# x in four large loads and transposed unscaled, and load buffers of w_ada and of the weights kept apart

## The chip, the cores and the metric

The kernel runs on one core of one Trainium2 chip. The metric is the device time of one execution in microseconds. The engines are TensorE (PE, with its weight loads as PEld), VectorE (DVE), ScalarE (ACT), GpSimd (POOL) and SyncE (SP), whose queue issues nearly all DMAs.

## The reference, cut to what matters

One decoder layer over x of 256 rows by 2048 columns, in float32:

```python
mod = jax.nn.silu(c) @ w_ada + b_ada                  # 2048 x 6144
shift, scale, gate = jnp.split(mod, 3, axis=-1)
h = _rms_norm(x, g_norm) * (1.0 + scale[:, None, :]) + shift[:, None, :]
proj = h @ w_in                                       # 2048 x 9296
qa, ka, va, za, q_idx, k_idx, w_idx, qb, kb, vb, zb = jnp.split(proj, COL_SPLITS, axis=-1)
...
ya = _dsa_attention(qa, ka, va, q_idx, k_idx, w_idx, _alibi_slopes(N_HEADS_A))
yb = _moba_attention(qb, kb, vb, _alibi_slopes(N_HEADS_B))
ya = ya.reshape(B, L, D_A) * jax.nn.silu(za)
yb = yb.reshape(B, L, D_B) * jax.nn.silu(zb)
y = jnp.concatenate([ya, yb], axis=-1) @ w_out        # 2048 x 2048
return x + gate[:, None, :] * y
```

Each of the two attentions has 8 heads of 128. The first attends to the top 64 keys of an indexer's score, the second is causal over the whole sequence.

## The kernel before

**Three matrix stages, one stream of loads.** w_ada (50 MB), w_in (76 MB) and w_out (17 MB) are each read once. A list `loads`, made by a planner at the top of the kernel, gives their order; SP issues them in it. A load of w_ada is a row of the transposed matrix for each of 128 partitions (128 x 2048, 1 MB): DVE multiplies it by `s_row` (the silu of c, the same in all partitions) and sums along the row (`gemv`, L274), which gives 128 values of shift, scale or gate. A load of w_in or w_out holds up to four k tiles (rows of 128) of one group of 512 columns (`za1`, `qb0`, ...; three groups `i0` to `i2` are narrower). A quad load holds one k tile of the four groups z, q, k, v of one half of the heads.

**Products in three passes.** Matmuls are done in a rounded float32 type. So each weight pair of k tiles is split: ACT rounds it (`wh`, L315, `cast_hi`), DVE subtracts that from the original (`wl`, L328, `cast_lo`), and PE adds three products for each k tile and each half t of the rows (L775 `wh` x `hhi`, L776 `wl` x `hhi`, L777 `wh` x `hlo`). The casts are written two pairs ahead of the matmuls (`LA`).

**h comes in chunks.** x is loaded, normalised by its row (`rx`), and transposed in 16 blocks of 128 columns (`xnT`). A chunk of one or two k tiles of h (`build_h`) needs two or four loads of w_ada; its ACT and DVE instructions make `hhi` and `hlo`. The planner places the w_ada loads at fixed distances, in k tiles of work (`ADA_NEXT`, `ADA_GAP`), and lets a projection start on the k tiles that are known, so that many groups are summed in several segments, each added to `p_...` by DVE or copied by ACT. Chunk 0 (k tile 0) starts the kernel: `start_mod` and a part of `build_h` turn five partial sums into its shift and scale.

**Buffers.** All loads share one ring of four buffers of 1 MB (`rawp`); a load is issued when the one four before it in the list has been read:

```python
raw = rawp.tile([P, 2048], F32, tag="raw", name=f"raw{n_issued}")
```

The rounded weights lie in two rings of four tiles, `wh` and `wl`. Numbers in names such as `raw6` are places in `loads`; numbers in `wh6` count pairs.

**Order.** A scheduler orders each engine's instructions by what it reckons, except inside `with in_order()`, which keeps the order of the code on each engine; the start is written so. Attention heads, gates and `build_h` are background steps that a small queue (`Bg`) mixes in between pairs. Each gate's `build_gate` waits some steps between its sum and its PE transposes (`yield 2`).

Of the kernel before, what the change touches and what calls it, by code (L numbers as in the profile page):

```python
# [13 lines left out]
P = 128  # L14
# [38 lines left out]
def hybrid_block(ctx: ExitStack, tc: tile.TileContext, x, cols, w_ada_t, w_in, w_out, out):  # L53
# [4 lines left out]
    rawp = ctx.enter_context(tc.tile_pool(name="rawp", bufs=4))  # L58
# [126 lines left out]
    while turn:  # L185
# [12 lines left out]
        if g[0] == "z" and end == seg0 + 1 and [pos[o] for o in gs] == 4 * [seg0]:  # L198
# [6 lines left out]
            first = len(loads) == len(PARTS)  # L205
            for lo, hi in ((0, 1), (1, 3), (3, 4)) if first else ((0, 2), (2, 4)):
                for i in range(lo, hi):
                    members[i]["pair"] = (lo, hi)
            loads.append(dict(kind="quad", quad=g[1:], k=seg0, members=members, first=first))
# [18 lines left out]
    for n, qs in seq:  # L228
        for q in qs:
            loads.append(w_load(w_out_r, f"o{n}", n * 512, 512, list(yk[q]), "y", q == QUADS[0],  # L230
                                q == QUADS[-1], True, True))

    n_start = 2 * CHUNKS[0][1]
    n_issued = 0

    def issue(upto):
        nonlocal n_issued
        while n_issued < min(upto, len(loads)):
# [27 lines left out]
    def gemv(ld):  # L266
# [15 lines left out]
    ada_done = []  # L282

# [535 lines left out]
```

## Time and profile before

| | |
|---|---|
| median of 3 runs | 585.94 us (584.33 to 586.25) |
| the profiled execution | 584.79 us, with a span of 583.0 us in the trace |
| granted TensorE clock, mean | 0.996 |
| PE / PEld / DVE / ACT / POOL busy | 554.7 / 458.2 / 451.8 / 318.6 / 49.3 us |
| DMA traffic | 150.08 MB, mean 257 GB/s |

The profiled execution is 1.79 us longer than its span (what lies around it), and 1.15 us shorter than the median. Busy time of PE is modelled: a matmul that waits in the array's queue counts as busy, so the count of matmuls in a stretch says more than its busy share.

### The profile page before, as it was taken

The page shows a single profiled execution, that of the slowest core. Times are in us where ns is not written, and L with a number is a line of the kernel's source. Part 1 is how long each engine was busy: PE and PEld are TensorE (multiplying, and loading weights), DVE is VectorE, ACT ScalarE, POOL GpSimd, SP SyncE. Part 2 cuts the span into 40 slices and gives each one's busy share as a digit, 9 for nine tenths or more (in the row PEclk, how much of TensorE's full clock was granted, in tenths as well). Part 3 has the DMA queues.
Part 4 walks back from the last instruction along what each step waited for, and adds up shares of the span by engine and source line. Part 5 has one row for each costly group of instructions (what it writes and reads, how often), then busy time and mean ns, then how long its engine had stood idle before and what let it go on. Part 6 is the DMA issues. An engine that isn't in the chain of part 4 may idle for free.

```text
span 583.0 us, 7393 instructions
## 1 busy us (share of the span) xinstructions
PE 554.7 (95%) x2626; PEld 458.2 (79%) x2626; DVE 451.8 (77%) x698; ACT 318.6 (55%) x648; POOL 49.3 (8%) x66
## 2 busy tenths in 40 slices
PE   4887999999999999999999998999999999999996
PEld 3666688878898888787776887888888888888885
DVE  4796689899988887979978899997587556557452
ACT  5766645353545352536588675657755775544340
POOL 5400000000000000010021120111101110000000
PEclk9999899999999999999999999999999999999999
DMA  8889898999899979898666465877495459445701
GB/s 278 336 280 330 327 335 273 345 327 360 308 359 329 389 290 333 317 310 311 223 216 215 148 217 184 320 247 255 170 341 181 144 171 332 147 145 195 238 37 36
DMA packets 59973, 150.08 MB, mean 257 GB/s; under 512 B 3104, under 2 KB 9504, under 8 KB 54048
## 3 DMA queue, kind: packets, MB, share of 16 engines
q1 hardware_dynamic: 58784, 147.51, 72.2%
q10 hardware_dynamic: 1152, 2.10, 1.2%
q8 instruction: 20, 0.33, 0.2%
q14 instruction: 17, 0.14, 0.1%
HBM read 147.50 MB, written 2.10 MB: 257 GB/s over the span
## 4 chain that ended last, share of the span: by engine, by line
PE 70%; DVE 12%; ACT 7%; DMA 5%; issue 3%; POOL 2%; SPq 0%; DVEq 0%; ACTq 0%
PE mm_y_o L775 5%; PE mm_y_o L777 5%; PE mm_y_o L776 5%; DVE wl L328 5%; DVE raw L274 3%; DMA raw<-in_w_in 3%; ACT wh L315 3%; PE mm_h_i L775 2%; PE mm_h_ka L775 2%; PE mm_h_va L777 2%; PE mm_h_va L776 2%; PE mm_h_qa L777 2%; PE mm_h_ka L777 2%; PE mm_h_ka L776 2%; PE mm_h_i L776 2%
## 5 line engine op out<-in xcount | busy, mean ns | idle before, releaser
L315 ACT ACTIVATE wh<-raw 128x1024 fp32r<-128x1024 f32 (+3 forms) x189 | 186.7, 1003 | 164.5 <-DMA raw<-in_w_in 58.3
L328 DVE TENSOR_TENSOR wl<-raw,wh 128x1024 fp32r<-128x1024 f32 (+3 forms) x189 | 214.6, 1153 | 71.5 <-ACT wh L315 70.8
L274 DVE CUSTOM_DVE_ANT_0 raw<-raw,s_row 128x2048 f32<-128x2048 f32 (+2 forms) x51 | 110.9, 2177 | 8.4 <-DMA raw<-in_w_ada_t 8.3
L775 PE MATMUL mm_y_o<-wh,yT 128*128 128x512 f32 x128 | 51.5, 403 | 0.0
L777 PE MATMUL mm_y_o<-wh,yT 128*128 128x512 f32 x128 | 49.9, 390 | 0.0
L776 PE MATMUL mm_y_o<-wl,yT 128*128 128x512 f32 x128 | 49.9, 390 | 0.0
L775 PE MATMUL mm_h_i<-wh,hhi 128*128 128x384 f32 (+1 forms) x96 | 32.0, 335 | 3.2 <-DVE p_i L684 2.0
L776 PE MATMUL mm_h_i<-wl,hhi 128*128 128x384 f32 (+1 forms) x96 | 31.6, 330 | 0.8 <-DVE wl L328 0.8
L777 PE MATMUL mm_h_i<-wh,hlo 128*128 128x384 f32 (+1 forms) x96 | 31.4, 329 | 0.0
L777 PEld LDWEIGHTS mm_y_o<-wh,yT 128*128 128x128 f32 x128 | 24.0, 188 | 5.3 <-DVE yT L582 0.2
L775 PEld LDWEIGHTS mm_y_o<-wh,yT 128*128 128x128 f32 x128 | 24.1, 188 | 4.8 <-ACT yT L581 0.2
L776 PEld LDWEIGHTS mm_y_o<-wl,yT 128*128 128x128 f32 x128 | 24.1, 188 | 4.6
L775 PE MATMUL mm_h_qa<-wh,hhi 128*128 128x512 f32 x64 | 26.2, 412 | 1.1 <-ACT p_za L682 1.1
L775 PE MATMUL mm_h_zb<-wh,hhi 128*128 128x512 f32 x64 | 25.6, 405 | 1.5 <-ACT wh L315 1.5
L776 PE MATMUL mm_h_zb<-wl,hhi 128*128 128x512 f32 x64 | 25.9, 404 | 0.7 <-DVE wl L328 0.7
L775 PE MATMUL mm_h_kb<-wh,hhi 128*128 128x512 f32 x64 | 25.9, 410 | 0.6 <-ACT wh L315 0.6
L775 PE MATMUL mm_h_ka<-wh,hhi 128*128 128x512 f32 x64 | 25.9, 407 | 0.0
L775 PE MATMUL mm_h_vb<-wh,hhi 128*128 128x512 f32 x64 | 25.9, 407 | 0.0
L777 PE MATMUL mm_h_za<-wh,hlo 128*128 128x512 f32 x64 | 25.0, 392 | 0.9 <-DVE hlo L424 0.9
L775 PE MATMUL mm_h_za<-wh,hhi 128*128 128x512 f32 x64 | 25.8, 408 | 0.0
L777 PE MATMUL mm_h_zb<-wh,hlo 128*128 128x512 f32 x64 | 25.7, 401 | 0.0
L776 PE MATMUL mm_h_kb<-wl,hhi 128*128 128x512 f32 x64 | 25.2, 393 | 0.5 <-DVE wl L328 0.5
(225 smaller groups left out, 1209.5 us busy)
## 6 DMA issues: line engine op xcount, KB each, us to landing
raw<-in_w_in SPq DMA_DIRECT2D x50, 1024.0 KB, 5.8
raw<-in_w_ada_t SPq DMA_DIRECT2D x46, 1024.0 KB, 6.2
raw<-in_w_out SPq DMA_DIRECT2D x16, 1024.0 KB, 5.0
raw<-in_w_in SPq DMA_DIRECT2D x18, 512.0 KB, 3.9
raw<-in_w_in SPq DMA_DIRECT2D x11, 768.0 KB, 5.9
x<-in_x SPq DMA_DIRECT2D x8, 256.0 KB, 5.0
xr<-in_x ACTq DMA_DIRECT2D x8, 256.0 KB, 7.7
raw<-in_w_in SPq DMA_DIRECT2D x3, 672.0 KB, 4.3
```

What stands on the lines that cost most here:

```text
L274: nc.vector.tensor_tensor_reduce(out=ld["v"][:, h0:h1], in0=ld["v"][:, h0:h1], in1=s_row[:, h0:h1], scale=1.0, scalar=0.0, op0=ALU.mult, o ...
L315: nc.scalar.activation(hi[:, :n, :w], v, AF.Copy)
L328: nc.vector.tensor_tensor(lo[:, :n, :w], v, sb["hi"][:, :n, :w].bitcast(F32), op=ALU.subtract)
L775: nc.tensor.matmul(ps, a_hi, sb["hi"][:, sb["i"] + i, :w], start=st, stop=False)
L776: nc.tensor.matmul(ps, a_hi, sb["lo"][:, sb["i"] + i, :w], start=False, stop=False)
L777: nc.tensor.matmul(ps, a_lo, sb["hi"][:, sb["i"] + i, :w], start=False, stop=en)
```

## The change

**Loads.** The one ring of 1 MB buffers becomes two: two of 1 MB for w_ada and four of 512 KB for weights. Every weight load is now at most one pair of k tiles (a quad becomes two loads, the first quad three), so that a load and its pair of casts are one to one; 156 loads become 237. `issue` no longer follows the list alone: it takes, of the kinds that have a free buffer, the load that stands first in the list; a w_ada load only if it is at most four places ahead. A weight buffer counts as free after its `cast_lo`, a w_ada buffer after the next `cast_hi` behind its `gemv`. The planner asks for w_ada loads between pairs, no longer between fours. `wh` and `wl` become two halves of one tile.

**x.** Four loads of 512 KB take the place of eight of 256 KB. ACT squares all of them (four instructions of 1024 columns); one `rsqrt` serves both halves of the rows. Only block 0 is scaled before its transposes; the other 15 are transposed as they are. `rx` is itself transposed and copied over all partitions (`r_bc`), and POOL multiplies blocks 1 to 15 by it (`x_norm`), in places spread over the first pairs (`X_AT`). Blocks 1 to 7 get a copy from PSUM by ACT there (`x_copy`), where before `build_h` read PSUM itself.

**Smaller.** Chunk 0's partial sums are joined by DVE alone, with one instruction behind the last sum, not three on POOL and one on DVE. `build_gate` waits eight steps, not two.

```diff
-    rawp = ctx.enter_context(tc.tile_pool(name="rawp", bufs=4))
+    rawp = ctx.enter_context(tc.tile_pool(name="rawp", bufs=1))
...
+    def w_tile(name):
+
+        return wsp.tile([P, 2, 2, 512], F32R, tag="w", name=name)
...
-        for k in range(seg0, end, 4):
-            n = min(4, end - k)
+        for k in range(seg0, end, 2):
+            n = min(2, end - k)
...
+    AHEAD = 4
+    kinds = {kind: [n for n, ld in enumerate(loads) if (ld["kind"] == "ada") == (kind == "ada")] for kind in ("ada", "w")}
+    free = {"ada": 2, "w": 4}
...
+    def issue():
+        while True:
+            ns = [kinds[kind][0] for kind in kinds if kinds[kind] and free[kind] > 0
+                  and (kind == "w" or kinds[kind][0] <= next_load + AHEAD)]
+            if not ns:
+                break
+            n_issued = min(ns)
             ld = loads[n_issued]
-            raw = rawp.tile([P, 2048], F32, tag="raw", name=f"raw{n_issued}")
...
+            if kind == "ada":
+                raw = ld["v"] = rawp.tile([P, D], F32, tag="ada", bufs=2, name=f"ada{n_issued}")
...
+                raw = rawp.tile([P, 1024], F32, tag="raw", bufs=4, name=f"raw{n_issued}")
...
+            for n, (h0, h1) in enumerate(parts[:-1]):
+                part(h0, h1, 2 + n)
+            more = acc[:, 3:4] if len(parts) > 2 else 0.0
+            nc.vector.scalar_tensor_tensor(acc[:, 4:5], acc[:, 2:3], more, bmod[:, i:i + 1], op0=ALU.add, op1=ALU.add)
+            part(*parts[-1], i)
+            nc.vector.tensor_scalar(acc[:, i:i + 1], acc[:, i:i + 1], acc[:, 4:5], gcol[:, 0:1] if i else 1.0,
+                                    op0=ALU.add, op1=ALU.mult)
...
+        while read:
+            free[read.pop()] += 1
+        issue()
         flush_gemv()
...
-        lo = wsp.tile([P, 2, 512], F32R, tag="wl", name=f"wl{j}")
-        nc.vector.tensor_tensor(lo[:, :n, :w], v, sb["hi"][:, :n, :w].bitcast(F32), op=ALU.subtract)
-        sb["lo"] = lo
+        nc.vector.tensor_tensor(sb["lo"][:, :n, :w], v, sb["hi"][:, :n, :w].bitcast(F32), op=ALU.subtract)
+        free["w"] += 1
+        issue()
...
+    xt = [w_tile(f"x{t}").rearrange("p c k n -> p (c k n)").bitcast(F32) for t in range(2)]
     for t in range(2):
-        for j in range(4):
-            xx = u_tile(f"x_{t}_{j}")
-            nc.sync.dma_start(xx, x[t * P:(t + 1) * P, j * 512:(j + 1) * 512])
-            xt.append(xx)
-    issue(n_start + 1)
+        for h in range(2):
+            nc.sync.dma_start(xt[t][:, h * 1024:(h + 1) * 1024], x[t * P:(t + 1) * P, h * 1024:(h + 1) * 1024])
+    issue()
...
+    def x_norm(k):
+
+        nc.gpsimd.tensor_tensor(xnT[k], xnT[k], r_bc, op=ALU.mult)
...
-        yield 2
+        yield 8
...
+        for t in range(2):
+            nc.scalar.activation(xt[t][:, :P], xt[t][:, :P], AF.Copy, scale=rx[:, t:t + 1])
+        for t in range(2):
+            for k in range(8, 16):
+                x_transpose(k, t)
+        for t in range(2):
+            x_transpose(0, t)
+        for k in (8, 9, 10, 11, 0, 12, 13, 14, 15):
             x_copy(k)
+        for k in range(1, 8):
+            for t in range(2):
+                x_transpose(k, t)
+        pr = mm_tile("prx")
+        for t in range(2):
+            nc.tensor.transpose(pr[:, t * P:(t + 1) * P], rx[:, t:t + 1].to_broadcast([P, P]), ident)
...
+    X_AT = {1 + 2 * (k - 1): k for k in range(1, KT)}
...
+        if j in X_AT:
+            with in_order():
+                if X_AT[j] < 8:
+                    x_copy(X_AT[j])
+                x_norm(X_AT[j])
```

What this moves shows at three places. On ACT, at the start, from the scaling of x to the first weights (`xnT8` is block 8 of x transposed, `hhi0` the first tile of h, `r_bc` the row factors, the last `raw` and `w` rows are the weights of the first quad); before:

```order
L366 ACTIVATE x_1_3_162<-x_1_3_162,rx_175 128x512
L385 ACTIVATE xnT0_249<-ptx0_209 128x256
L385 ACTIVATE xnT8_251<-ptx4_215 128x256
...
L385 ACTIVATE xnT11_257<-ptx5_218 128x256
L315 ACTIVATE wh0_274<-raw2_171 128x512
L417 ACTIVATE hhi0_279<-xnT0_249,mmod0_259 128x256
L385 ACTIVATE xnT12_285<-ptx6_221 128x256
...
L385 ACTIVATE xnT15_291<-ptx7_224 128x256
L315 ACTIVATE wh1_293<-raw2_171 128x1024
```

and now:

```order
L638 ACTIVATE x1_149<-x1_149,rx_170 128x128
L387 ACTIVATE xnT8_208<-ptx4_185 128x256
...
L387 ACTIVATE xnT11_214<-ptx5_188 128x256
L387 ACTIVATE xnT0_216<-ptx0_205 128x256
L387 ACTIVATE xnT12_218<-ptx6_191 128x256
...
L387 ACTIVATE xnT15_224<-ptx7_194 128x256
L344 ACTIVATE w0_258<-raw2_161 128x512
L411 ACTIVATE hhi0_263<-xnT0_216,mmod0_246 128x256
L659 ACTIVATE r_bc_171<-prx_243 128x256
L344 ACTIVATE w1_272<-raw3_163 128x1024
```

All nine copies stand ahead of `hhi0`, and a copy of `r_bc`, which needs the last transposes of PE, stands between `hhi0` and the second weights.

On SP, the loads behind the first quad (a row that reads `in_w_ada_t` is a load of w_ada; the group of the next weights, `za1`, is `raw6` before and `raw9` now); before:

```order
L252 DMA raw3_268<-in_w_in 128x4x512
L244 DMA raw4_270<-in_w_ada_t 128x2048
L244 DMA raw5_272<-in_w_ada_t 128x2048
L260 DMA raw6_325<-in_w_in 128x2x512
L260 DMA raw7_383<-in_w_in 128x2x512
L244 DMA raw8_385<-in_w_ada_t 128x2048
L260 DMA raw9_387<-in_w_in 128x2x512
L244 DMA raw10_416<-in_w_ada_t 128x2048
L260 DMA raw11_434<-in_w_in 128x2x512
L260 DMA raw12_436<-in_w_in 128x2x336
```

and now:

```order
L260 DMA ada7_256<-in_w_ada_t 128x2048
L275 DMA raw6_261<-in_w_in 128x2x512
L260 DMA ada8_270<-in_w_ada_t 128x2048
L275 DMA raw9_275<-in_w_in 128x2x512
L275 DMA raw10_295<-in_w_in 128x2x512
L275 DMA raw12_312<-in_w_in 128x2x512
L275 DMA raw14_344<-in_w_in 128x2x512
L275 DMA raw15_379<-in_w_in 128x2x336
L260 DMA ada11_403<-in_w_ada_t 128x2048
L260 DMA ada13_405<-in_w_ada_t 128x2048
```

Five weight loads now stand ahead of the third and fourth w_ada load of this stretch (`ada11` and `ada13`, which were `raw8` and `raw10`), where one and two stood before.

On DVE, the same stretch (L274 and L289 are the products with w_ada, `hlo1` is the rest of the second tile of h, L328 and L354 the second casts); before:

```order
L328 TENSOR_TENSOR wl9_420<-raw7_383,wh9_418 128x1024
L408 TENSOR_TENSOR mmod1_389<-mmod1_389,cc_76 128x1
L680 COPY p_za0_1_432<-mm_h0_za0_1_423 128x512
L274 ISA raw8_385,mmod2_438<-raw8_385,s_row_110 128x2048
L274 ISA mmod2_438 128x1
L424 TENSOR_TENSOR hlo1_414<-xnT1_411,hhi1_410 128x256
L328 TENSOR_TENSOR wl10_442<-raw9_387,wh10_440 128x1024
```

and now:

```order
L679 COPY p_za0_1_422<-mm_h0_za0_1_413 128x512
L404 TENSOR_TENSOR mmod1_373<-mmod1_373,cc_76 128x1
L354 TENSOR_TENSOR w9_407<-raw10_295,w9_407 128x1024
L354 TENSOR_TENSOR w10_426<-raw12_312,w10_426 128x1024
L417 TENSOR_TENSOR hlo1_398<-xnT1_289,hhi1_395 128x256
L354 TENSOR_TENSOR w11_455<-raw14_344,w11_455 128x1024
L289 ISA ada11_403,mmod2_424<-ada11_403,s_row_110 128x2048
```

`hlo1` no longer stands behind the product with that w_ada load, and two casts have moved ahead of it.

## Rows read from the trace of the kernel before

**Rows 1.** The page: the chain that ended last, share of the span by engine.

```profile
PE 70%; DVE 12%; ACT 7%; DMA 5%; issue 3%; POOL 2%; SPq 0%; DVEq 0%; ACTq 0%
```

**Rows 2.** Windows: stretch, length, busy (count) by engine, PEclk, DMA share, GB/s.

```profile
21.60:40.00 18.40, 16.84 (x68) 12.23 (x68) 15.60 (x19) 14.45 (x26) 0.00 (x0) 1.00 0.75 266
40.00:56.00 16.00, 13.69 (x64) 10.93 (x64) 11.86 (x13) 10.27 (x18) 0.00 (x0) 1.00 0.92 323
56.00:70.00 14.00, 11.19 (x39) 8.03 (x38) 8.90 (x13) 9.09 (x14) 0.00 (x0) 0.88 1.01 389
70.00:130.00 60.00, 59.96 (x263) 49.21 (x263) 55.19 (x66) 29.11 (x39) 0.00 (x0) 1.00 0.89 310
...
250.00:350.00 100.00, 95.40 (x497) 76.92 (x496) 85.43 (x177) 66.21 (x184) 14.67 (x13) 1.00 0.68 232
```

**Rows 3.** The same view of three shorter stretches.

```profile
11.00:25.00 14.00, 9.96 (x42) 7.45 (x40) 10.07 (x20) 7.96 (x19) 7.42 (x8) 1.00 1.03 406
25.00:31.00 6.00, 6.00 (x28) 4.96 (x28) 5.62 (x6) 5.94 (x12) 0.00 (x0) 1.00 0.36 116
31.00:37.00 6.00, 4.85 (x22) 3.62 (x20) 6.00 (x9) 4.13 (x7) 0.00 (x0) 1.00 0.85 268
```

**Rows 4.** Timeline of SP's queue: start, length, what it issued.

```profile
25.85 4.67 SPq L260 DMA_DIRECT2D raw<-in_w_in  x2
31.28 0.34 SPq L244 DMA_DIRECT2D raw<-in_w_ada_t  x1
```

**Rows 5.** Timeline of the start: start, length, instruction, [idle before <-releaser].

```profile
14.88 1.33 ACT L366 ACTIVATE x<-x,rx 128x512 f32<-128x512 f32 x2 [3.40 <-POOL rx L139]
...
15.78 1.57 DVE L274 CUSTOM_DVE_ANT_0 raw<-raw,s_row 128x1024 f32<-128x1024 f32 x1
...
18.50 2.82 PE L377 MATMUL ptx<-ident,x 128*128 128x128 f32 x12 [0.19 <-POOL x L368]
18.91 0.08 DVE L274 DVE_READ_ACCUMULATOR2_ANT mmod<- 128x1 f32 x1
...
20.96 0.60 ACT L417 ACTIVATE hhi<-xnT,mmod 128x256 fp32r<-128x256 f32 x1
...
21.61 0.50 PE L775 MATMUL mm_h_qb<-wh,hhi 128*128 128x512 f32 x1 [0.30 <-ACT hhi L417]
...
23.66 0.73 PE L775 MATMUL mm_h_kb<-wh,hhi 128*128 128x512 f32 x2 [0.35 <-ACT wh L315]
```

**Rows 6.** Groups of instructions by form, 20 to 70 us: busy us, mean ns | idle before.

```profile
L274 DVE CUSTOM_DVE_ANT_0 raw<-raw,s_row 128x2048 f32<-128x2048 f32 x7 | 16.0, 2289 | 4.2 <-DMA raw<-in_w_ada_t 4.2
L328 DVE TENSOR_TENSOR wl<-raw,wh 128x1024 fp32r<-128x1024 f32 x12 | 14.5, 1222 | 7.0 <-ACT wh L315 7.0
L315 ACT ACTIVATE wh<-raw 128x1024 fp32r<-128x1024 f32 x12 | 12.6, 1062 | 2.4 <-DMA raw<-in_w_in 2.4
```

**Rows 7.** What PE waited for, 21.6 to 70 us, then 250 to 360: total, times, longest.

```profile
PE mm_h_zb L775 <- ACT wh L315: 1.5, 1, 1.5
...
PE mm_h_za L777 <- DVE hlo L424: 0.9, 1, 0.9
...
PE pgate L435 <- DVE ygb L578: 1.5, 1, 1.5
```

**Rows 8.** Timeline of DVE around the second tile of h.

```profile
38.13 2.29 DVE L274 CUSTOM_DVE_ANT_0 raw<-raw,s_row 128x2048 f32<-128x2048 f32 x1 [1.06 <-DMA raw<-in_w_ada_t]
...
40.35 0.42 DVE L424 TENSOR_TENSOR hlo<-xnT,hhi 128x256 fp32r<-128x256 f32 x1
```

**Rows 9.** Groups by form, 0 to 22 us: POOL's scaling of x, ACT's copies of blocks.

```profile
L368 POOL TENSOR_SCALAR x<-x,rx 128x512 f32<-128x512 f32 x3 | 4.7, 1573 | 0.0
...
L385 ACT ACTIVATE xnT<-ptx 128x256 f32<-128x256 f32 x8 | 2.5, 382 | 2.6 <-PE ptx L377 2.6
```

**Rows 10.** DMA issues, 70 to 250 us: count, KB each, median us to landing.

```profile
raw<-in_w_in SPq DMA_DIRECT2D x20, 1024.0 KB, 6.2
...
raw<-in_w_in SPq DMA_DIRECT2D x5, 512.0 KB, 5.4
```

More of the change, by code (lines that the diff above doesn't have):

```diff
@@ L204, in hybrid_block @@
                               end == KT) for c in "qkvz"]
-            first = len(loads) == len(PARTS)
-            for lo, hi in ((0, 1), (1, 3), (3, 4)) if first else ((0, 2), (2, 4)):
+            for lo, hi in ((0, 1), (1, 3), (3, 4)) if len(loads) == len(PARTS) else ((0, 2), (2, 4)):
                 for i in range(lo, hi):
-                    members[i]["pair"] = (lo, hi)
-            loads.append(dict(kind="quad", quad=g[1:], k=seg0, members=members, first=first))
+                    members[i]["i"] = i - lo
+                loads.append(dict(kind="quad", quad=g[1:], k=seg0, members=members[lo:hi], lo=lo, hi=hi))
             n_kt += 4
@@ L229, in hybrid_block @@
         for q in qs:
-            loads.append(w_load(w_out_r, f"o{n}", n * 512, 512, list(yk[q]), "y", q == QUADS[0],
-                                q == QUADS[-1], True, True))
+            for k in yk[q][::2]:
+                loads.append(w_load(w_out_r, f"o{n}", n * 512, 512, [k, k + 1], "y",
+                                    q == QUADS[0] and k == yk[q][0], q == QUADS[-1] and k == yk[q][2], True, True))
     n_start = 2 * CHUNKS[0][1]
[L234 to L238, printed above, removed]
-            ld = loads[n_issued]
-            raw = rawp.tile([P, 2048], F32, tag="raw", name=f"raw{n_issued}")
-            if ld["kind"] == "ada":
-                ld["v"] = raw
+    AHEAD = 4
@@ L270, in gemv, with part @@
             mod[kind, c] = work.tile([P, 8], F32, name=f"m{kind}{c}", tag="m" + kind)
-        for n, (h0, h1) in enumerate(ld.get("parts", [(0, D)])):
-            o = i if (kind, c) != ("mod", 0) else 2 * i + n
+        acc = mod[kind, c]
+        def part(h0, h1, o):
             nc.vector.tensor_tensor_reduce(out=ld["v"][:, h0:h1], in0=ld["v"][:, h0:h1], in1=s_row[:, h0:h1],
                                            scale=1.0, scalar=0.0, op0=ALU.mult, op1=ALU.add,
-                                           accum_out=mod[kind, c][:, o:o + 1])
-            if (kind, c, o) == ("mod", 0, 3):
-                start_mod()
+                                           accum_out=acc[:, o:o + 1])
+        parts = ld.get("parts")
+        if parts:
+            for n, (h0, h1) in enumerate(parts[:-1]):
[5 more added lines that the diff above has]
+                                    op0=ALU.add, op1=ALU.mult)
+        else:
+            part(0, D, i)
+        read.append("ada")
         if "end" in ld:
@@ L282, in hybrid_block @@
     ada_done = []
+    read = []
     subs = []
@@ L380, in hybrid_block, with x_transpose @@
-    for k in range(8):
-        xnT[k] = None
+        for h in range(2):
+            nc.sync.dma_start(xt[t][:, h * 1024:(h + 1) * 1024], x[t * P:(t + 1) * P, h * 1024:(h + 1) * 1024])
+    issue()
+    ssx = consts.tile([P, 2, 2], F32, name="ssx")
+    rx = consts.tile([P, 2], F32, name="rx")
+    r_bc = h_tile("r_bc")
+    xnT, ptx = {}, {}
+    def x_transpose(k, t):
+        k2, i = k // 2, k % 2
+        if k2 not in ptx:
+            ptx[k2] = ps_tile(("tr", "s", "pt", "pv")[k2], f"ptx{k2}") if k2 < 4 else mm_tile(f"ptx{k2}")
+        o = i * L + t * P
+        src = xt[t][:, k * P:(k + 1) * P]
+        nc.tensor.transpose(ptx[k2][:, o:o + P], src, ident)
@@ L659, in hybrid_block @@
             pass
-        for k in range(12, 16):
-            x_copy(k)
+        nc.scalar.activation(r_bc, pr[:, :L], AF.Copy)
     ada_done.remove(0)
@@ L678, in evac @@
                     proj[g, t] = u_tile(f"p_{g}_{t}")
-                    if "pair" in ld and t == 1 and ld["i"] == 1:
+                    if t == 1 and ld.get("i") == 1:
                         nc.vector.tensor_copy(proj[g, t][:, :w], ps[:, :w])
```

106 lines of the change are left out of this document (30 added, 76 removed).

## The prediction

> **What bounds the kernel now.** I read four views in this order. First the page's chain that ended last: PE carries 70% of it, DVE 12%, ACT 7%, DMA 5% [rows 1], so most of the time goes with PE's own pace, and a gain has to come from places where PE is not at work. The windows by stage say where those are. From 70 to 130 us PE has 263 matmuls in 60 us, one each 0.228 us, with no idle time [rows 2]; there nothing can be won but by PE. Between 21.6 and 70 us it has only 171 in 48.4 us [rows 2]. Of these, 36 are of the narrow groups i0 to i2 (three pairs of 12, 336 and 384 columns of 512, so about 0.165 us each); the rest at 0.228 gives 30.8 + 5.9 = 36.7 us. So 11.7 us are lost there, after the 21.6 us before the first product, and these two are what a change of the start can reach. Of the 11.7, some 1.7 are no wait: the granted clock has a mean of 0.88 from 56 to 70 us [rows 2], which is 12% of 14 us, so for a part of it the clock was at its lower level of 1.2 GHz, right behind PE's longest wait of the stretch, 1.5 us for the first cast of zb [rows 7].
>
> The third view is that of the DMAs in the same stretch. From 11 to 25 us they move 406 GB/s, then 116 up to 31 us and 268 up to 37 [rows 3]. SP shows why: its next weights go out only at 25.85 us, and the next load of w_ada at 31.28 [rows 4], since all four buffers are held by loads that have landed and wait for their casts. In those 12 us 2.3 MB moved where 4.9 could have, which is 6.3 us of transfer. The fourth view, DVE's and ACT's waits of 20 to 70 us, shows the bill: 4.2 us of waiting for w_ada and 2.4 for weights [rows 6].
>
> **The change, part by part.** *Start.* x has the same bytes and the same last landing, and ACT squares the last 1024 columns in about the time that DVE took; so I leave `rx` at 14.9 us, where ACT's scaling begins now [rows 5]. Then ACT scales two blocks (0.6), copies blocks 8 to 11 and 0 (five at no more than 0.38 [rows 9], 1.7 us): 17.2. The other transposes share a PSUM bank with block 0 and follow its copy: 14, and two of `rx`, at 2.82 / 12 = 0.235 us [rows 5], 3.8 us: 21.0. The first product, 21.61 now [rows 5], moves by 0.6. Chunk 0's numbers would be there earlier: the three POOL steps between the last sum at 18.99 and `hhi` at 20.96 go [rows 5], about 1.7 us, and that lead is lost behind the transposes. Next come the copy of `r_bc` (0.38) and the second weights' cast (1.06 [rows 6]), 22.4 for 23.66 [rows 5]. **-1.2 us**, between -2.0 and 0.
>
> *Loads.* The two rings take the first quads as four loads beside two of w_ada, and three pairs of weights follow as each small load is cast, not as a whole megabyte is. So weights of za1, qa1, ka1 stand in line 5 to 10 us before they do now, and `ada11` and `ada13` behind them. Two places gain. `hlo1` stands behind a product with w_ada that began late at 38.13 us, and starts at 40.35 [rows 8], while PE waits for it [rows 7]. It now stands behind one cast more and not behind that product: DVE is free at 38.13 - 1.06 = 37.07 [rows 8], one cast takes 1.22 [rows 6], so `hlo1` starts near 38.3: **-2.0 us** (0 if that cast's data are late, -3.3 if it is done before). And the weights of zb are in line before the last w_ada load of the next chunk, so the wait of 1.5 us and the lower clock behind it (1.7) should go: **-3.2 us** (0 to -8, all else that is lost up to 70 us).
>
> Loads of half the size cost 81 more issues on SP, of 0.34 us as the single one in [rows 4], spread over 570 us of a queue that mostly waits; nothing of it is late unless a load is. A 512 KB load took 5.4 us to land beside others, a 1024 KB one 6.2 [rows 10]; for bytes that is much worse, but several are in flight. A ring of four turns once in 5.4 + 1.06 + 1.22 + one product with w_ada in DVE's way, 2.29 [rows 6, 10] = 10.0 us; PE needs 4 x 12 x 0.228 = 10.9 us for four loads. Covered, by 0.9: **0**. The Trainium skill, DMA: Bandwidth & Descriptors, "Rules for kernel authors", asks for at least 1 MiB for each DMA. Its fixed 2.0 us a DMA ("Anatomy of one DMA") would be, as an estimate from that page, 162 us for 81 more loads if none overlapped and the sum near 740; the trace agrees on the direction (5.4 is far more than half of 6.2), not on the price, as loads overlap.
>
> *POOL's multiplies.* 15 new instructions of 128 x 256 with two inputs, between 23 and about 60 us. No row shows one. Beside POOL's scaling of x (1.57 us each [rows 9]) DVE's product of 1024 columns took 1.57 us [rows 5] where half of one of 2048 is 1.14 [rows 6]: 0.4 us of delay. I take that for each, the nearest row: 6.3 us of DVE. DVE is idle for 18.4 - 15.6 + 16 - 11.9 + 14 - 8.9 = 12 of the 48.4 us [rows 2], but not where the chain of w_ada, casts and h runs through it; I put a fifth on the path, **+1.2 us**, between 0 and 15 x 1.57 - 12 = 11.6. The Trainium skill, SBUF — State Buffer, "Who interferes with whom", says that a DVE instruction with two inputs in SBUF and a POOL instruction that reads SBUF lock each other out for a whole instruction. The trace agrees (1.57 against 1.14).
>
> *ACT* gets eight copies of 0.38 in place of five scalings: nothing, as it is idle for a quarter of that time [rows 2]; without that cover, 3 us.
>
> *Later.* Up to 250 us the order of loads is that of the list. From 250 to 350 us, 12 products for the gates stand before cast 133, where eight did, and DVE is busy for 85 of 100 us there [rows 2]; against that, the gates' transposes come six steps later, and PE now waits 1.5 us for one [rows 7]. **0**, between -1.5 and +2.3 (one product in a tight place).
>
> Sum: -1.2 - 2.0 - 3.2 + 1.2 = -5.2 us. The profiled execution, 584.8, would be 579.6; the median stands 1.15 above it: **580.7 us**, between 574 (all but a little of what is lost won) and 584.
>
> **The rivals.**
> 1. *Given back.* PE comes to 70 us five earlier, but DVE has 55 of 60 us of work there [rows 2], and every product with w_ada must come as much earlier. If DVE or the loads cannot, PE waits until it is where it was: 585, no change. For it: PE's waits end just as DVE saturates. Against it: DVE's idle 12 us before are what the earlier data fill.
> 2. *The ring is too short (slower).* All the weights in flight are 2 MB; before, up to four. Place: 70 to 240 us. If landings beside w_ada take 7.5 us and not 5.4, the ring turns in 12.1 us against 10.9, 11% of 170 us, 18 us lost: 599. It decides from a landing of 6.7 us on ((6.7 + 4.57 - 10.9) / 10.9 x 170 = 5.8, about the gain). For it: 6.2 us for the large ones [rows 10], and segments of five k tiles that split 2, 2, 1. Against it: w_ada no longer holds these buffers, and they come free after one cast, not two. By the rule of the Trainium skill on the size of a DMA (DMA: Bandwidth & Descriptors, "Rules for kernel authors") this rival is the one to expect.
> 3. *POOL's lock (slower).* If each multiply stops DVE for 1.57 us and DVE's idle time is all the cover, 11.6 us stand against 6.4: 591. It decides from (12 + 6.4) / 15 = 1.2 us each. Against it: the 0.4 seen, at twice the columns.
>
> **How the numbers follow.** A median of this kernel's runs can tell about 0.3%, 1.8 us, from no change. Forecast 0.62, given back 0.16, short ring 0.12, lock 0.10. All of the forecast's range is faster, both last rivals are mostly slower: faster 0.62, same 0.16, slower 0.22. 574 to 588 holds nearly all of the first two and the near part of the slower ones, about 0.8; the forecast's own range is 574 to 584.
>
> **What would show it.** Start: the first product near 21.0 us, the second group near 22.4. Loads: DMA from 25 to 37 us above 300 GB/s; `hlo1` near 38.3; no wait at zb and a granted clock of 1.00 from 50 to 70 us; more than 190 matmuls up to 70 us. Ring: from 70 to 240 us one matmul each 0.228 us as now, and 512 KB loads landing in under 6.7 us. Lock: DVE's products between 25 and 60 us not much over 2.7 us. It would be wrong if PE began to wait for casts after 70 us, if transposes of x held the first products past 21.6, or if the third and fourth load of w_ada, now behind five of weights, made the chunk after the second late enough that zb's wait only moves to qb.

## The result, and the profile after

The changed kernel takes 591.52 us (median of 4 runs, 589.81 to 593.28), the kernel before 585.56 us beside it. The ratio is 1.0104, with a 95% interval from 1.0080 to 1.0128: 6.1 us slower, where 580.7 us and faster were forecast. The profiled execution took 589.81 us, with a span of 588.0 us. The chain of the page has moved from PE towards the others, against [rows 1]:

```profile
PE 64%; DVE 13%; ACT 10%; issue 4%; DMA 4%; POOL 3%; SPq 0%; ACTq 0%; DVEq 0%
```

The windows by stage, as in [rows 2] (busy time and count of PE, PEld, DVE, ACT and POOL, granted clock, DMA share, GB/s), and under them those of [rows 3]:

```profile
21.60:40.00 18.40, 16.95 (x70) 12.38 (x69) 16.70 (x18) 16.56 (x31) 8.00 (x5) 1.00 0.83 310
40.00:56.00 16.00, 13.74 (x67) 11.23 (x65) 15.25 (x13) 8.92 (x18) 16.00 (x9) 1.00 0.96 354
56.00:70.00 14.00, 12.18 (x44) 9.28 (x45) 10.41 (x12) 7.68 (x12) 1.41 (x3) 0.88 0.77 267
70.00:130.00 60.00, 58.36 (x256) 47.39 (x255) 54.97 (x68) 28.22 (x37) 0.00 (x0) 1.00 0.93 329
250.00:350.00 100.00, 91.91 (x466) 73.30 (x465) 86.48 (x175) 63.62 (x178) 16.82 (x12) 0.98 0.69 228
...
11.00:25.00 14.00, 10.78 (x43) 8.13 (x44) 11.18 (x23) 10.54 (x26) 1.91 (x4) 0.76 1.03 404
25.00:31.00 6.00, 5.58 (x25) 4.21 (x23) 6.00 (x5) 4.95 (x10) 3.82 (x2) 1.00 0.84 288
31.00:37.00 6.00, 4.96 (x20) 3.13 (x19) 5.38 (x10) 5.33 (x10) 0.23 (x1) 1.00 0.62 221
```

Up to 70 us the change does gain: 181 matmuls from 21.6 us on, where there were 171, and some ten products lie before 21.6 us, where the kernel before had none. DMA from 25 to 37 us moves 254 GB/s, where it was 192. Then the gain goes. From 250 to 350 us PE has 466 matmuls, where it had 497. The start, to be read with [rows 5]:

```profile
11.60 0.73 POOL L143 TENSOR_TENSOR rx<-rx,mhalf 128x2 f32<-128x2 f32 x1
12.36 0.69 ACT L638 ACTIVATE x<-x,rx 128x128 f32<-128x128 f32 x2 [1.31 <-POOL rx L143]
...
14.47 3.25 PE L383 MATMUL ptx<-ident,x 128*128 128x128 f32 x14 [0.89 <-ACT xnT L387]
...
17.63 0.27 DVE L301 TENSOR_SCALAR mmod<-mmod,cc 128x1 f32<-128x1 f32 x1
...
18.00 0.60 ACT L411 ACTIVATE hhi<-xnT,mmod 128x256 fp32r<-128x256 f32 x1 [0.80 <-DVE mmod L301]
...
18.65 0.50 PE L781 MATMUL mm_h_qb<-w,hhi 128*128 128x512 f32 x1 [0.50 <-ACT hhi L411]
```

The first product stands at 18.65 us, 2.96 us earlier, and waits for chunk 0's scale, not for transposes. PE has only two matmuls from 11 to 14.4 us, and the clock falls: it is 0.50 from 14.4 to 18 us, the level of 1.2 GHz, where [rows 3] have 1.00 from 11 to 25. The 14 transposes there take 0.232 us each even so, about as in [rows 5].

A count of PE's matmuls by stage tells where the time went later, 0.228 us each for those of 512 columns (from the windows of each run; the kernels have the same ones in each stage but for what is early or late, and kernels with the new x have two more transposes up to 70 us):

| PE matmuls in | 0-70 us | 70-250 | 250-285 | 285-330 | 330-475 | 475-500 |
|---|---|---|---|---|---|---|
| before | 218 | 825 | 182 | 217 | 709 | 120 |
| changed | 238 | 826 | 178 | 189 | 709 | 112 |

Twenty more up to 70 us, 28 fewer from 285 to 330 us (6.4 us), eight fewer from 475 to 500 us (1.8 us). In the first of these losses lie the attention's index scores (`lg`, `rl`) and the factors of q and k (`ss..`). PE's and ACT's waits of 285 to 330 us in the changed kernel (total, times, longest):

```profile
PE lg L474 <- ACT qi L468: 2.6, 2, 1.9
PE pgate L428 <- ACT rl L477: 1.8, 1, 1.8
PE sb L540 <- ACT rl L477: 1.8, 1, 1.8
ACT p_qb L513 <- POOL ssqb L143: 6.9, 2, 4.2
ACT p_kb L513 <- POOL sskb L143: 2.2, 1, 2.2
```

and the first and fourth of these in the kernel before:

```profile
PE lg L481 <- ACT qi L475: 1.1, 1, 1.1
ACT p_qb L520 <- POOL ssqb L139: 2.4, 2, 2.0
```

ACT scales q only when POOL has made its factors in two small steps, and stands still until then; behind it wait `qi` and `rl`, and for these PE. (PE's wait at `pgate` is not POOL's: it is 1.8 us in run 11 too, where POOL has no part.) POOL's steps and what DVE did beside them, from the timelines of the changed kernel:

```profile
293.51 2.56 POOL L142 TENSOR_SCALAR ssqb<-ssqb 128x8 f32<-128x8 f32 x1 [35.82 <-ACT jqb L506]
296.16 1.64 POOL L143 TENSOR_TENSOR ssqb<-ssqb,mhalf 128x8 f32<-128x8 f32 x1
...
319.71 0.70 POOL L142 TENSOR_SCALAR ssqb<-ssqb 128x8 f32<-128x8 f32 x1 [12.98 <-ACT jqb L506]
320.50 3.62 POOL L143 TENSOR_TENSOR ssqb<-ssqb,mhalf 128x8 f32<-128x8 f32 x1
...
293.73 2.28 DVE L289 CUSTOM_DVE_ANT_0 ada<-ada,s_row 128x2048 f32<-128x2048 f32 x1
...
320.35 2.28 DVE L289 CUSTOM_DVE_ANT_0 ada<-ada,s_row 128x2048 f32<-128x2048 f32 x1
```

and POOL's same steps in the kernel before:

```profile
296.48 0.20 POOL L138 TENSOR_SCALAR ssqb<-ssqb 128x8 f32<-128x8 f32 x1 [35.35 <-ACT jqb L513]
296.77 1.66 POOL L139 TENSOR_TENSOR ssqb<-ssqb,mhalf 128x8 f32<-128x8 f32 x1
...
319.80 1.28 POOL L138 TENSOR_SCALAR ssqb<-ssqb 128x8 f32<-128x8 f32 x1 [12.38 <-ACT jqb L513]
321.16 1.64 POOL L139 TENSOR_TENSOR ssqb<-ssqb,mhalf 128x8 f32<-128x8 f32 x1
```

A step of 0.20 us takes 2.56 us and ends at 296.07 us, right behind a gate's product with w_ada that runs until 296.01; the second takes 3.62 us beside the next such product. In the kernel before, the products of the gates stood elsewhere, and of these four steps one was held, for 1.28 us, up to the end of a pair of DVE's casts (321.08 and 321.02 us). As the prediction read from the order, twelve gate products now stand ahead of cast 133, where eight did.

### The profile page after: what moved, and what is told of

Its sections match the earlier page's. It is cut to its first block, busy times and chain, and to the rows that moved or that the text cites. A ratio compares the mean times of both kernels' runs of the same rounds, so it can differ in the third digit from the quotient of the medians.

```text
span 588.0 us, 7642 instructions
## 1 busy us (share of the span) xinstructions
PE 558.2 (95%) x2628; PEld 459.0 (78%) x2628; DVE 454.5 (77%) x696; ACT 319.3 (54%) x649; POOL 70.2 (12%) x73
## 4 chain that ended last, share of the span: by engine, by line
PE 64%; DVE 13%; ACT 10%; issue 4%; DMA 4%; POOL 3%; SPq 0%; ACTq 0%; DVEq 0%
DVE w L354 5%; PE mm_y_o L782 5%; PE mm_y_o L783 5%; PE mm_y_o L781 5%; ACT w L344 3%; DVE ada L289 3%; DMA ada<-in_w_ada_t 3%; PE mm_h_qb L782 2%; PE mm_h_qa L782 2%; PE mm_h_qa L783 2%; PE mm_h_qb L783 2%; PE mm_h_qb L781 2%; PE mm_h_qa L781 2%; PE mm_h_i L782 2%; PE mm_h_i L781 2%
## 5 line engine op out<-in xcount | busy, mean ns | idle before, releaser
L354 DVE TENSOR_TENSOR w<-raw,w 128x1024 fp32r<-128x1024 f32 (+3 forms) x189 | 218.6, 1171 | 71.1 <-ACT w L344 70.5
L344 ACT ACTIVATE w<-raw 128x1024 fp32r<-128x1024 f32 (+3 forms) x189 | 187.8, 1003 | 156.1 <-DMA raw<-in_w_in 51.5
L289 DVE CUSTOM_DVE_ANT_0 ada<-ada,s_row 128x2048 f32<-128x2048 f32 (+2 forms) x51 | 111.6, 2189 | 2.8 <-DMA ada<-in_w_ada_t 2.7
L781 PE MATMUL mm_y_o<-w,yT 128*128 128x512 f32 x128 | 51.4, 403 | 0.2 <-ACT w L344 0.2
L782 PE MATMUL mm_y_o<-w,yT 128*128 128x512 f32 x128 | 50.0, 391 | 0.8 <-DVE w L354 0.8
L783 PE MATMUL mm_y_o<-w,yT 128*128 128x512 f32 x128 | 50.0, 390 | 0.0
L781 PE MATMUL mm_h_i<-w,hhi 128*128 128x384 f32 (+1 forms) x96 | 32.0, 337 | 1.2 <-DVE p_i L683 0.8
L782 PE MATMUL mm_h_i<-w,hhi 128*128 128x384 f32 (+1 forms) x96 | 31.9, 332 | 0.6 <-DVE w L354 0.6
L782 PEld LDWEIGHTS mm_y_o<-w,yT 128*128 128x128 f32 x128 | 24.1, 188 | 5.7 <-DVE w L354 1.1
L781 PEld LDWEIGHTS mm_y_o<-w,yT 128*128 128x128 f32 x128 | 24.1, 188 | 5.4 <-ACT w L344 0.6
L783 PEld LDWEIGHTS mm_y_o<-w,yT 128*128 128x128 f32 x128 | 24.0, 188 | 5.2 <-DVE yT L575 0.2
L781 PE MATMUL mm_h_qb<-w,hhi 128*128 128x512 f32 x64 | 25.9, 411 | 2.1 <-ACT w L344 1.6
L782 PE MATMUL mm_h_za<-w,hhi 128*128 128x512 f32 x64 | 25.2, 394 | 1.8 <-DVE w L354 1.8
L782 PE MATMUL mm_h_qb<-w,hhi 128*128 128x512 f32 x64 | 25.7, 402 | 0.9 <-DVE w L354 0.9
L781 PE MATMUL mm_h_vb<-w,hhi 128*128 128x512 f32 x64 | 26.5, 420 | 0.0
L781 PE MATMUL mm_h_za<-w,hhi 128*128 128x512 f32 x64 | 26.0, 412 | 0.3 <-ACT w L344 0.3
L782 PE MATMUL mm_h_vb<-w,hhi 128*128 128x512 f32 x64 | 25.7, 402 | 0.4 <-DVE w L354 0.4
L782 PE MATMUL mm_h_zb<-w,hhi 128*128 128x512 f32 x64 | 25.1, 392 | 1.0 <-DVE w L354 1.0
L781 PE MATMUL mm_h_zb<-w,hhi 128*128 128x512 f32 x64 | 25.4, 400 | 0.5 <-ACT w L344 0.5
```

The lines of the kernel that those rows point to most:

```text
L344: nc.scalar.activation(sb["hi"][:, :n, :w], v, AF.Copy)
L354: nc.vector.tensor_tensor(sb["lo"][:, :n, :w], v, sb["hi"][:, :n, :w].bitcast(F32), op=ALU.subtract)
L781: nc.tensor.matmul(ps, a_hi, sb["hi"][:, sb["i"] + i, :w], start=st, stop=False)
L782: nc.tensor.matmul(ps, a_hi, sb["lo"][:, sb["i"] + i, :w], start=False, stop=False)
L783: nc.tensor.matmul(ps, a_lo, sb["hi"][:, sb["i"] + i, :w], start=False, stop=en)
```

## The experiments

Theory A, after this reading: gate products that now run beside POOL's steps for the attention hold POOL up, ACT waits for POOL, and PE for ACT. Rival B: the gates' transposes, eight steps behind their sums and not two. Rival C: the loss was made before 250 us, by POOL's multiplies of x or by the loads of half the size.

**1. Gate products back.** Each gate's product may not run before the cast behind which it ran in the kernel before.

```diff
+    PIN = (87, 92, 96, 100, 104, 106, 109, 118, 122, 125, 128, 131, 134, 137, 143, 147)
...
+            if at >= 0 and at not in lo_ins:
+                break
...
+            if at >= 0:
+                tc.add_manual_dep(nc.cur_bb.bb.instructions[n], lo_ins[at].name, NO_WAIT, reason="pin")
```

> The changed kernel with one thing undone: each product with w_ada that makes a gate may not run on DVE before the second cast behind which it ran in the kernel before (casts 87 to 147); data, loads and all else as changed. Theory A (the 7 us lost between 290 and 330 us come from gate products that now run beside POOL's two short steps of rsqrt, hold POOL up, and with it ACT and PE): PE's waits at 298 us (1.85) and 323 us (1.8) go, the granted clock stays 1.00 from 300 to 305 us (0.69 in the changed kernel), POOL's pairs of rsqrt steps for qb take about 2 and 3 us, not 4.3 each; time 591.5 - 5 = 586.5 us. Rival B (the gate's transposes, eight steps behind and not two, disturb PE and the order): no change, 590 to 593. Rival C (the loss was made before 250 us, by the multiplies on POOL and the half-size loads): no change, 590 to 593.

Measured: 585.84 us, ratio to the kernel before 1.0001 (0.9982 to 1.0020), against 1.0104: 1.03%, 6.0 us, came back. From 285 to 330 us there are 203 matmuls, not 189, and from 250 to 285 us 188, not 178: together 24, or 5.5 us. ACT's waits for POOL's `ssqb` fall from 6.9 to 3.7 us, and in POOL's timeline the second pair of steps takes 1.9 us, not 4.4:

```profile
317.06 0.20 POOL L142 TENSOR_SCALAR ssqb<-ssqb 128x8 f32<-128x8 f32 x1 [14.87 <-ACT jqb L516]
317.34 1.64 POOL L143 TENSOR_TENSOR ssqb<-ssqb,mhalf 128x8 f32<-128x8 f32 x1
```

That the places of these products cost 6 us is shown. The clock did not go as expected (0.96 over the stage, as in the changed kernel): PE now waits 2.3 us for the first gate's transposes.

**2. and 3. The gates' transposes two steps behind again,** alone, and with the products held back.

```diff
-        yield 8
+        yield 2
```

> The changed kernel with the gate's transposes two steps behind its sum again, not eight. Theory A: the wait of 1.8 us at 311 us for the transposes of the first gate goes or shrinks to the 0.4 us of before, the waits at 298 and 323 us stay: 591.5 - 1.4 = 590. Rival B: all of the 7 us between 290 and 330 us come back, 585. Rival C: no change.

> Both together: gate products no earlier than before, and their transposes two steps behind. Theory A: the two gains add up, 591.5 - 6.5 = 585, and from 250 to 400 us as much is lost as in the kernel before. Rival C: 590 to 593.

Measured: 591.94 us alone, ratio 1.0106 (1.0072 to 1.0139), no gain; 585.24 us with both, ratio 1.0000 (0.9982 to 1.0018), no more than the products gave. Rival B falls, and the 1.4 us that theory A gave to the transposes do not show in the time. Run 2's trace, of the fastest of its six executions (587.86 us), has 216 matmuls from 285 to 330 us, as many as before, but 687 from 330 to 475 us, where there were 709. There PE waits for the second gate instead:

```profile
PE pgate L428 <- DVE ygb L571: 4.0, 1, 4.0
```

ACT's wait for `ssqb` is only 2.4 us in this trace, with the gate products still early, and `ygb` stands on DVE right behind one of them (346.66 to 348.93 us). So this trace suggests that an early product can hurt by DVE's own time as well; no run tests that apart. In run 3's trace PE is nine matmuls (2 us) ahead of run 1's at 475 us, and falls behind up to 500 us (99, where run 1 has 112), while ACT waits 5.5 us for a load of w_out. So the earlier transposes may gain something before 475 us; none of it is kept.

**4. The old x,** eight loads, scaled by ACT and POOL, with the loads and gates of the change.

> The changed kernel with x loaded, scaled by ACT and POOL and transposed as before (eight loads, no POOL multiplies; the joined sums of chunk 0 stay). If the new x is worth what its trace shows at the start (first product 18.65 against 21.61 us) and its multiplies cost DVE little, this is slower than the changed kernel by up to 3 us: 594. If the multiplies that hold POOL without a gap from 37 to 57 us cost as much on DVE (its products with w_ada take 2.82 us there, not 2.29, and PE waits 1.0, 1.6 and 0.9 us and has half its clock for 5 us), the loss at the start comes back by 65 us: 590 to 592, with no wait over 1 us from 50 to 60 us. What is lost from 290 to 330 us stays in both.

Measured: 587.90 us, ratio 1.0035 (1.0014 to 1.0055), 0.69% or 4.0 us faster than with the new x. That is neither of the two expected times. The first product comes at 20.57 us, 1.9 us later than in the changed kernel, and yet there are 249 matmuls up to 70 us, not 238.

**5. The new x without its multiplies.**

```diff
                 if X_AT[j] < 8:
                     x_copy(X_AT[j])
-                x_norm(X_AT[j])
```

> The changed kernel without POOL's 15 multiplies: blocks 1 to 15 of x stay unnormalised, all other work is as in the changed kernel. Theory A (with the old x the same loads bring PE to 65 us some 2.5 to 3 us earlier than with the new one, because the multiplies stretch DVE's instructions): DVE's products with w_ada between 40 and 58 us take 2.29 us, not 2.82, its casts 1.22, not 1.45 to 1.71; the wait of 1.0 us for zb at 51 us goes; PE at 65 us is 6 to 8 us ahead of the kernel before, not 3.5; time 591.5 - 3.5 = 588. Rival (the multiplies lie in DVE's idle time; what the old x gained there came from its other order): no change, 590 to 593.

Measured: 588.28 us, ratio 1.0045 (1.0028 to 1.0063), 0.59% or 3.5 us less than the changed kernel; 250 matmuls up to 70 us. DVE's groups by form from 40 to 58 us, first of the changed kernel:

```profile
L289 DVE CUSTOM_DVE_ANT_0 ada<-ada,s_row 128x2048 f32<-128x2048 f32 x4 | 10.8, 2688 | 0.5 <-DMA ada<-in_w_ada_t 0.5
L354 DVE TENSOR_TENSOR w<-raw,w 128x1024 fp32r<-128x1024 f32 x2 | 3.3, 1630 | 0.8 <-ACT w L344 0.8
L354 DVE TENSOR_TENSOR w<-raw,w 128x768 fp32r<-128x768 f32 x2 | 2.9, 1486 | 0.0
```

and without the multiplies:

```profile
L289 DVE CUSTOM_DVE_ANT_0 ada<-ada,s_row 128x2048 f32<-128x2048 f32 x4 | 9.1, 2287 | 1.0 <-DMA ada<-in_w_ada_t 1.0
L354 DVE TENSOR_TENSOR w<-raw,w 128x1024 fp32r<-128x1024 f32 x2 | 2.5, 1225 | 3.5 <-ACT w L344 3.5
L354 DVE TENSOR_TENSOR w<-raw,w 128x768 fp32r<-128x768 f32 x2 | 1.9, 958 | 0.5 <-ACT w L344 0.4
```

Each DVE instruction of these rows loses 0.4 to 0.5 us beside the multiplies, 12 of which run without a gap from 36.8 to 57.4 us (20.64 us in one row of POOL's timeline, 1.72 us each; the very first, at 21.55 us, took 0.74). Of rival C this part is true: 3.5 us. And since the run with the old x and this one are 0.1% apart (249 matmuls up to 70 us, and 250 with two transposes more), the earlier first product is worth nothing at the end.

**6. The old x with the gate products back.**

> The old x (587.9) and the gate products held behind the casts of before, with the loads of the change. If the two losses are independent, 587.9 - 5.7 = 582.2, which would be the loads' own worth: 3.6 us faster than the kernel before. If the lead at 65 us is spent elsewhere (waits of the stage of the attention that end when PE is ahead), 585.

Measured: 582.53 us, ratio 0.9951 (0.9933 to 0.9969). The two losses are independent as far as the intervals can tell: the gate products are worth 0.84% here and 1.03% with the new x. What is left of the change, its loads, the joined sums of chunk 0 and the later transposes of the gates, with the loss of run 7 still in it, is worth 2.9 us.

**7. The output's loads of x spread.** ACT issues eight loads of x for the output at the start of the last stage. In the changed kernel its queue stops in the midst of them; the timeline of ACT:

```profile
481.58 8.67 ACTq L748 DMA_DIRECT2D xr<-in_x  x2
490.30 0.47 ACT L534 ACTIVATE qka<-tra,gnega 128x256 f32<-128x256 f32 x1 [7.86 <-DMA raw<-in_w_out]
```

The kernel before issues the same eight loads at once, but the same two took

```profile
478.82 2.92 ACTq L742 DMA_DIRECT2D xr<-in_x  x2
```

and ACT's longest wait from 475 to 500 us was 3.0 us.

```diff
-        if ld["kset"] == "y" and "xload" not in started:
...
+        if ld["kset"] == "y" and len(xr) < 8:
+            n, t = divmod(len(xr), 2)
+            xr[n, t] = u_tile(f"xr{n}{t}")
+            nc.scalar.dma_start(xr[n, t], x[t * P:(t + 1) * P, n * 512:(n + 1) * 512])
```

> The changed kernel with the gate products held back (585.84), and the eight loads of x for the output issued by ACT one behind each of the first eight pairs of w_out, not all at once. In the changed kernel ACT's seventh of these issues waits from 482 to 489.9 us, the moment at which a load of w_out lands, and ACT does nothing in 7.9 us; PE then waits for casts at 490 to 493 us. Theory D (the issue on ACT waits for the weight load that last used its semaphore): ACT's idle time of 7 us goes, what PE loses from 450 to 500 us falls from 4.4 to 2.6 us, 585.8 - 1.8 = 584. Rival (the first loads of w_out are late by themselves): no change, 585 to 587.

Measured: 582.98 us, ratio 0.9963 (0.9947 to 0.9980), 0.38% or 2.2 us less than run 1. From 475 to 500 us there are 123 matmuls, not 112 (2.5 us), and ACT's wait of 7.9 us is gone; its longest there is 2.3 us. That the wait goes when the issues are spread is shown. The burst alone does not make it: the kernel before has it without the wait, and in run 11 five of its issues took 3.14 us. What in the changed kernel makes it longer stays open; that it is a semaphore shared with a load of w_out is argued from the profile's releaser alone.

**8. x normalised in its transposes,** by a product with a diagonal matrix of the row factors, so that POOL has no multiplies.

```diff
-        nc.tensor.transpose(ptx[k2][:, o:o + P], src, ident)
+        nc.tensor.matmul(ptx[k2][:, o:o + P], src, rdiag[t], start=True, stop=True)
```

> The gate products held back (585.84), and x normalised in its transposes: PE multiplies each block by a diagonal matrix of the row factors, so POOL has no multiplies; 24 blocks' halves stand before the first products, 8 behind the first group. Theory A: the first product stays near 18.6 us (24 x 0.235 = 5.6 from about 12.9), DVE's products take 2.29 us, PE at 65 us is 7 us ahead of the kernel before, not 3.3; time 585.8 - 3.5 = 582.3. Rival: products of a diagonal take longer than transposes and push the first product past 20 us; 584 to 586.

Measured: 584.14 us, ratio 0.9985 (0.9964 to 1.0005): the rival's case. All products must wait for `rx`; each is two matmuls in the trace, the first 26 (52 matmuls) take 8.41 us, up to 18 us mostly at 1.2 GHz (granted clock 0.54 from 11 to 18 us), and the first product of weights comes at 20.84 us. A difference of 0.16% from run 1 is within the intervals. DVE's products take 2.29 us again, but at the end ACT's wait of run 7 is 8.3 us, and there are 102 matmuls from 475 to 500 us, with a granted clock of 0.93.

**9. and 10. The losses removed together,** with the new x (its row factors applied by DVE where a tile of h is made) and with the old one.

```diff
-                nc.scalar.activation(xnT[k], xnT[k], AF.Identity, bias=sh, scale=am)
-                nc.scalar.activation(hhi[k], xnT[k], AF.Copy)
+                nc.vector.scalar_tensor_tensor(xnT[k], xnT[k], am, r_bc, op0=ALU.mult, op1=ALU.mult)
+                nc.scalar.activation(hhi[k], xnT[k], AF.Identity, bias=sh)
```

> The changed kernel with the gate products held back and the x loads of the output spread (583.0), and the row factors applied where a tile of h is made: one DVE instruction of 128 x 256 multiplies by scale and row factors in place of ACT's scaling, ACT adds the shift in its rounding, DVE in its subtraction. POOL's 15 multiplies go, the early start stays, DVE has 15 instructions of some 0.42 us more, one at a time over 270 us. Theory A: the 3.2 us of the multiplies come back, less about one half of 15 x 0.42 = 6.3 us where DVE is full: 583.0 - 3.2 + 1.5 = 581, at best 579.8. Rival: from 70 to 250 us DVE has no room for it, and PE waits for casts there: 584 or more.

> The loads of the change with the old x, the gate products held back (582.5), and the x loads of the output spread. Gains independent: 582.5 - 2.9 = 579.6, less if the wait at 485 us is only partly of that cause: 581.

Measured: 580.04 us, ratio 0.9891 (0.9857 to 0.9925), and 579.70 us, ratio 0.9902 (0.9870 to 0.9934). Both are faster than both kernels, by some 1% than the one before. They are equal within their intervals, so here too the new x, with its row factors on DVE, gains nothing over the old. No run spreads the loads of x in the kernel before, where it may gain something too. The windows of the first of them:

```profile
0.00:70.00 70.00, 57.65 (x257) 45.72 (x258) 53.57 (x76) 48.51 (x87) 6.42 (x26) 0.98 0.92 343
70.00:250.00 180.00, 177.45 (x821) 149.07 (x821) 163.12 (x198) 74.09 (x86) 0.00 (x0) 1.00 0.90 325
250.00:285.00 35.00, 34.22 (x188) 28.48 (x187) 32.45 (x50) 20.23 (x37) 0.90 (x2) 1.00 0.90 317
285.00:330.00 45.00, 42.72 (x218) 33.19 (x217) 39.64 (x90) 33.59 (x107) 7.09 (x7) 1.00 0.57 189
```

**11. and 12. POOL out of the attention's chain,** in the changed kernel and in the one before. Experiment 1 moved DVE's work and the loads (185 GB/s from 285 to 330 us, 234 in the changed kernel) as well as POOL's, so it can't tell whether the product hurts by holding POOL up or by its own 2.3 us on a full DVE. Here the products stay, and both kernels leave out the power -1/2 of the attention's factors.

```diff
+        if n == HD:
+            nc.scalar.activation(dst, ssq, AF.Copy, scale=1.0 / n)
+            return
```

> The changed kernel, but the factors of the attention's q and k are one small ACT instruction in place of POOL's two: the power -1/2 is left out there. Gate products stand where the change puts them. Theory A (the gate products do their harm by holding POOL up, and ACT behind it): the waits of ACT for POOL (6.9 + 2.2 us from 285 to 330 us) go, PE's waits at 298 and 323 us with them, and the changed kernel comes within 1.5 us of the next kernel. Rival (they harm by DVE's own time in a full stage): PE's waits there stay, and it stays 5 us above the next kernel.

> The kernel before with the same edit, as the control: POOL's steps take 2 to 3.7 us a pair there and PE has few waits on them, so theory A expects 1 to 2 us less than the kernel before, 584; the rival the same. What tells the two apart is the distance of the run before this to this one, against the 5.96 us between the two kernels as they are.

Measured: 580.78 us, ratio 0.9898 (0.9862 to 0.9934), and 581.06 us, ratio 0.9919 (0.9890 to 0.9948). The 6 us between the two kernels are gone when POOL is out of the chain. The kernel before gains 0.81%, 4.7 us, where 1 to 2 were expected, so POOL's steps cost it more than was read from its waits. The window of 285 to 330 us, changed and before:

```profile
285.00:330.00 45.00, 43.20 (x220) 33.10 (x219) 43.77 (x88) 36.35 (x114) 1.42 (x1) 1.00 0.77 260
```

```profile
285.00:330.00 45.00, 44.61 (x226) 34.22 (x225) 41.02 (x85) 37.21 (x115) 0.51 (x1) 1.00 0.60 212
```

DVE is fuller than ever (43.77 of 45 us, with the gate products in it), and PE has 220 matmuls. So in this stretch it was POOL, not DVE's time. A caution on the size: in this run the loss of run 7 at the end is gone too (123 matmuls from 475 to 500 us). The distance of the ratios went from +1.04% to -0.21%; of these 1.25%, give or take 0.5, up to 0.38% may be that, and some 0.87%, 5.1 us, are POOL's.

## Why the prediction was wrong

**The step that failed** is "Later. 0, between -1.5 and +2.3 (one product in a tight place)". It counted the gate products that come earlier and looked at DVE's time alone. Two losses stand there instead: 6.0 us by the products' places (run 1), through POOL and ACT (runs 11 and 12), and 2.2 us by the loads of x at the end (run 7), where the kernel before has no such wait. Together they are 8.2 us. The prediction had seen that twelve products come before cast 133 where eight did; what was not asked is which POOL instructions stand beside them, and who waits for those. The gates' transposes six steps later, the other part of this step, gave no time back (runs 2 and 3). The prediction used the lock for x's multiplies and not for POOL's other work.

**POOL's multiplies, +1.2 us:** the mechanism was right, the size was not: 3.5 us (run 5). The delay for each DVE instruction was right (0.4 taken, 0.40 for a product and 0.41 for a cast of 1024 columns in run 5's rows), and so was their number, roughly: the eight instructions of those rows lose 3.5 us from 40 to 58 us, three smaller ones another 1.3, where 6.3 were taken for all. The fifth on the path was wrong: DVE is busy for 15.25 of 16 us there, so most of it counts. Rival 3's 591 us is near the measured time by chance: its multiplies cost a third of what it said.

**Start, -1.2 us:** the first product came 2.96 us earlier, not 0.6, because `rx` is there at 12.36 us; I had left it at 14.9. All sums stand on ACT now, and POOL's power took 0.73 us where the second one before took 1.57 beside a DVE product. But 2 us more or less at the first product are worth nothing at the end (runs 4 and 5, 9 and 10).

**Loads, -2.0 and -3.2 us:** `hlo1` stands at 36.35 us, earlier than the 38.3 forecast. The second term came only in part: in the changed kernel PE waits 1.0 us at zb and 1.6 us at qb, and the clock from 56 to 70 us is 0.88 as in [rows 2]. Without the multiplies qb's wait of 1.6 us stays, so it did move to qb, as the prediction's last sentence had it; but the clock is 1.00 from 56 to 70 us, with 56 matmuls where the changed kernel has 44. DMA from 25 to 37 us stayed under the 300 GB/s that were to show the gain. With the losses removed, the loads and chunk 0's sums are worth some 5.7 us (run 10: 0.98%, with whatever the spread loads of x gain), near the 5.2 forecast for the loads.

**Loads of half the size, 0:** right. From 70 to 250 us there are 826 matmuls and there were 825, and a load of 512 KB lands in 5.7 us, under the 6.7 of rival 2, at 335 GB/s in all, where there were 326:

```profile
raw<-in_w_in SPq DMA_DIRECT2D x47, 512.0 KB, 5.7
```

The Trainium skill's rule on the size of a DMA (DMA: Bandwidth & Descriptors, "Rules for kernel authors") asks for at least 1 MiB for the most bandwidth; runs 6 and 10, with 81 more loads than before, are faster than before, so for this kernel the measurement decides against it.

**Given back by 70 us (rival 1):** not so. Up to 285 us the changed kernel has done 1242 matmuls (238 + 826 + 178), the one before 1225, a lead of 15 without the two transposes more; it is lost behind that.

The sum closes: the forecast without its 1.2 us for POOL was -6.4 us; plus 6.0, 3.5 and 2.2 us that is +5.3, and +6.1 was measured. That it closes is in part luck: the 1.2 us of the start in it are worth nothing at the end, and each of the three losses is known only to some 1.5 us either way.

## What to carry to other kernels

An instruction that a scheduler is free to take forward must be judged by what it will run beside, not by its engine's free time: DVE products of two SBUF inputs next to POOL steps of 8 columns cost 6 us, because ACT and PE stood behind those steps. When buffers are split and loads come earlier, look up where their consumers go, and pin those that would land beside a short chain across engines. A gain at the start is only worth what the next bound lets through: here 2 us at the first product were gone at 70 us.

## What the runs showed of the hardware

A POOL instruction on 128 x 8 values, 0.20 us alone, took 2.56 us and ended with the DVE product beside it, and one of 1.64 us took 3.62. The Trainium skill, SBUF — State Buffer, "Who interferes with whom", has them lock each other out for a whole instruction; the trace agrees, however small POOL's work is.

ACT's issue of a small load stood still for 8 us (481.58 + 8.67, the changed kernel's rows under experiment 7) until, by the profile's releaser, a load of w_out on SP's queue had landed, and ACT's arithmetic stood behind it. Spread out, the same eight issues cost no such wait.

In experiment 8, transposing half a block by a product with a diagonal matrix took two matmuls in the trace. Windows of that run, first at 1.2 GHz for most of the time, then at 2.4, and one of the changed kernel:

```profile
12.46:18.00 5.54, 5.54 (x28) 5.54 (x29) 5.05 (x14) 1.94 (x6) 0.00 (x0) 0.55 1.05 397
18.00:20.80 2.80, 2.80 (x26) 2.68 (x24) 0.47 (x1) 2.34 (x7) 0.00 (x0) 1.00 0.97 393
...
14.40:18.00 3.60, 3.53 (x16) 3.27 (x16) 3.40 (x12) 1.75 (x7) 0.00 (x0) 0.50 1.07 403
```

Half a block took 0.40 us at the lower clock and 0.22 us at the higher. A transpose with the identity is one matmul, and took 0.232 us at 0.50 (14 in 3.25 us, in the rows of the start) and 0.235 at 1.00 [rows 5]: the lower clock slowed the products and not the transposes.
